# Sums of weight blocks: from VectorE to accumulating DMAs, and more pairs computed with them

## The chip, the core and the metric

The kernel runs on one core of one Trainium2 chip. The metric is the device time of one execution in microseconds (us), the median of several runs. TensorE (PE in the rows) multiplies, VectorE (DVE) and ScalarE (ACT) work element by element, GpSimd (POOL) does a few small sums and powers, and SyncE (SP) issues nearly all loads.

## The reference

Two layers of a decoder trunk over 512 tokens of width 1024. Each layer is a half-step SwiGLU, a mixing stage (sliding-window attention beside gated linear attention), and a second half-step SwiGLU. So there are four feed-forward stages, and the change is in them:

```python
def swiglu(h, w_gate, w_up, w_down):
    return (jax.nn.silu(h @ w_gate) * (h @ w_up)) @ w_down

h = rmsnorm(x, ffn1_norm[l])
x = x + 0.5 * swiglu(h, ffn1_w_gate[l], ffn1_w_up[l], ffn1_w_down[l])
...
h = rmsnorm(x, ffn2_norm[l])
x = x + 0.5 * swiglu(h, ffn2_w_gate[l], ffn2_w_up[l], ffn2_w_down[l])
```

The hidden width is 2816, that is 22 blocks of 128 columns.

## The kernel before

**Precision.** Everything is float32. TensorE is fed pairs of a rounded part and a rest: `split` has ACT round a 128x512 piece (line 112, `whi<-raw`) and DVE subtract (line 113, `wlo<-raw,whi`). `mul3` (lines 182 to 184) makes one product of three matmuls: high by high, high by low, low by high.

**The feed-forward stage.** `ffn` goes through 22 pairs `j`; a pair is 128 gate columns and 128 up columns of the weights, both over 1024 rows. Two halves, `h = 0` with pairs 0 to 10 and `h = 1` with pairs 11 to 21, are each followed by eight blocks of the down projection (`wd`). A pair is computed in one of two ways:

- `plain`: 8 row blocks, gate and up, three matmuls each: 48 matmuls with 128x512 outputs.
- `combined`: a Strassen-like scheme (Winograd's form) over rows, columns and tokens. Seven products, each of 4 row blocks and three matmuls on half of the tokens: 84 matmuls with 128x256 outputs. The activations' sums are made once per stage by `Norm.combine`; the weights' sums are made for each pair in `Combined`.

`PLAIN` names the pairs that are computed plainly: nine of 22.

**Weights of a combined pair.** `Combined` loads the pair's 128x2048 block into `raw` (two 512 KB loads on SP's queue) and cuts it in four: `g0`, `u0`, `g1`, `u1` (gate and up, even and odd row blocks). Each product needs one piece: 1 is `g0`, 2 is `g1`, 4 is `u1`, and 5, 6, 7 and 3 are sums and differences, which DVE makes in place inside `raw` by four tensor instructions (lines 166, 168, 171, 173). `raw` has two buffers, so the load of a pair waits until the last piece of the pair two before it has been split. `whi` and `wlo` have six buffers each: a new piece can be split only when TensorE has used up the piece six before.

**Order.** A scheduler fixes the order of the instructions on each engine when the kernel is built; a queue then runs in that order, and an instruction that waits holds up all behind it. `tc.high_priority(offset=PREP)` moves the preparation of weights ahead. TensorE's order within combined pairs is: product 1 of this pair, 4 of the pair before, 5 of this, 3 of the pair before, then 6, 2 and 7 of this. ACT copies product 1, 1+6 and 7 out (lines 363, 369, 375), takes the SiLU (line 319) and rounds the result (line 112, `q<-t` or `k<-t`); DVE adds (lines 373, 376, 383) and multiplies (386, 387).

The three lines on which most of this rests:

```python
raw = wpool.tile([P, 2048], F32, name="raw", tag="raw", bufs=2)
return [wpool.tile([P, 512], F32R, name=z, tag=z) for z in ("whi", "wlo")]
wpool = ctx.enter_context(tc.tile_pool(name="wpool", bufs=6))
```

Of the kernel before, what the change touches and what calls it, by code (L numbers as in the profile page):

```python
# [14 lines left out]
ALU = mybir.AluOpType  # L15
# [29 lines left out]

H = T // 2

PLAIN = (0, 1, 2, 3, 4, 8, 11, 15, 19)

VB = 144  # L50
VCUT = (0, 400, 784, 1168)
# [3 lines left out]
def trunk(ctx, tc, xT, wgu, wd, wqk, wv, wg, wpa, wpb, wo, glaw, vecs, consts, masks, out):  # L55
# [91 lines left out]
    class Combined:  # L147
# [3 lines left out]
        def __init__(self, src):  # L151
            self.of = {}

            def parts(product, r):
                self.of[product] = piece()
                split(*(z.rearrange("p (k c) -> p k c", k=4) for z in self.of[product]), r)

            with tc.high_priority(offset=PREP):
                raw = wpool.tile([P, 2048], F32, name="raw", tag="raw", bufs=2)
                for c in range(0, 2048, 1024):  # L160
                    nc.sync.dma_start(raw[:, c:c + 1024], src[:, c:c + 1024])

                r = raw.rearrange("p (k a n c) -> p k a n c", k=4, a=2, n=2)
                g0, u0, g1, u1 = (r[:, :, a, n, :] for a in range(2) for n in range(2))
                parts(1, g0)
                V.tensor_add(u0, u0, u1)
                parts(5, u0)
                V.tensor_sub(g0, u0, g0)
                parts(6, g0)
                parts(2, g1)  # L170
                V.tensor_sub(u0, u1, g0)
                parts(7, u0)
                V.tensor_sub(g1, g1, g0)
                parts(4, u1)
                parts(3, g1)

        def at(self, product, pair):
            return [z[:, pair * P:pair * P + P] for z in self.of[product]]
# [28 lines left out]
    class Norm:  # L207
# [14 lines left out]
        def whole(self, d):  # L222

            if d % 2 == 0:
                self.w = slot(f"{sets[1]}{d // 2}", (P, 2, T))
            t = self.w[:, d % 2, :]
            V.scalar_tensor_tensor(t, x[d], col(self.l, self.vcol + d), self.rb, op0=ALU.mult, op1=ALU.mult)  # L227
            split(*self.u[d], t)
            self.full.append(t)

        def combine(self, n):

            a, b = 2 * n, 2 * n + 1
            a0, a1, b0, b1 = (self.full[z][:, c:c + H] for z in (a, b) for c in (0, H))
            t, s = temp(2), temp(2)
            V.tensor_sub(t[:, :H], a1, a0)  # L236
            V.tensor_sub(t[:, H:], b1, t[:, :H])  # L237
            V.tensor_sub(s[:, :H], b1, a1)  # L238
            V.tensor_sub(s[:, H:], b0, t[:, H:])
            if n < 3:  # L240
                tags = (("b0", "b1"), ("qr0", "qr1"), ("ga", "gb"))[n]
                to = [[z[:, i, :] for i in range(2)] for z in (slot(v, (P, 2, T), F32R) for v in tags)]
            else:
                to = [[slot(v, dtype=F32R) for v in tags] for tags in (("attn0", "ke0"), ("attn1", "ke1"))]
            split(*to[0], t)
            split(*to[1], s)
            first, second = slice(0, H), slice(H, T)
            self.c.append({1: [z[:, first] for z in self.u[a]], 2: [z[:, first] for z in self.u[b]],
                           3: [z[:, second] for z in self.u[b]], 4: [z[:, second] for z in to[1]],
                           5: [z[:, first] for z in to[0]], 6: [z[:, second] for z in to[0]],  # L250
                           7: [z[:, first] for z in to[1]]})
# [40 lines left out]
    def ffn(f, norm, nxt, spill, last):  # L292
        for h in range(2):
            g = []

            rest = []
            room = {}

            def left(n=2):
                while n and rest:  # L300
                    rest.pop(0)()
                    n -= 1

            def part(tag, n):

                if tag not in room:
                    room[tag] = slot(tag, (P, 2, T), F32R)
                return room[tag][:, n, :]

            def keep(j, tu):  # L310
                if j < 8:
                    hi, lo = slot(f"{'qk'[j % 2]}{j // 2}", dtype=F32R), part(f"v{j // 2}", j % 2)
                else:
                    hi, lo = (part(f"{sets[1]}{2 * z + (j - 8) // 2}", j % 2) for z in range(2))
                split(hi, lo, tu)
                g.append((hi, lo))

            def silu(to, z):
                tables[0] = S.activation(to, z, AF.Silu)

            def plain(j):
                raw = h == 0 and j < 3
                w = first if f + h + j == 0 else Weights(wgu[f, h * NH + j], KD, 256)
                pg, pu = acc(), acc()
                for k in range(KD):
                    if h == 0 and j == 1 and k == 2:
                        norm.scale()
                    if h == 0 and j == 1 and k == 6:
                        norm.spread()
                    if k in (2, 5):  # L330
                        left(1)
                    mul3(pg, w.at(k, 0, P), norm.u[k], k == 0, k == KD - 1)
                    mul3(pu, w.at(k, P, P), norm.u[k], k == 0, k == KD - 1)
                    if h == 0 and j == 2:
                        norm.whole(k)
                    if h == 0 and j in (3, 4) and k in (3, 7):
                        norm.combine(2 * j - 6 + k // 4)

                def gated():
                    tg, tu = temp(1), temp(2)  # L340
                    if raw:
                        V.tensor_mul(tg, pg, norm.rb)
                        V.tensor_mul(tu, pu, norm.rb)
                        silu(tg, tg)
                        V.tensor_mul(tu, tu, tg)
                    else:
                        silu(tg, pg)
                        V.tensor_mul(tu, pu, tg)  # L348
                    keep(j, tu)

                return gated

            def combined(j):
                w = Combined(wgu[f, h * NH + j])

                def run(to, n, start=False):
                    for k in range(4):
                        mul3(to, w.at(n, k), norm.c[k][n], start and k == 0, k == 3, not start)

                a = acc()[:, :H]  # L360
                run(a, 1, True)
                s12 = temp(1)
                S.copy(s12[:, :H], a)
                left(1)
                b = acc()[:, :H]
                run(b, 5, True)
                left(1)
                run(a, 6)
                S.copy(s12[:, H:], a)
                c = psum()[:, :H]  # L370
                run(c, 2, True)
                tg, su = temp(1), temp(2)
                V.tensor_add(tg[:, :H], c, s12[:, :H])
                run(a, 7)
                S.copy(su[:, :H], a)
                V.tensor_add(su[:, H:], b, su[:, :H])

                def up():
                    run(a, 4)

                def gate():
                    run(b, 3)
                    V.tensor_add(tg[:, H:], b, s12[:, H:])
                    silu(tg, tg)
                    tu = temp(2)
                    V.tensor_mul(tu[:, :H], a, tg[:, :H])
                    V.tensor_mul(tu[:, H:], su[:, H:], tg[:, H:])
                    keep(j, tu)

                rest.extend((up, gate))  # L390

            late = None
            for j in range(NH):
                if h * NH + j in PLAIN:
                    gated = plain(j)
                    if h == 0 and j == 0:
                        late = gated
                    else:
                        if late is not None:
                            late()  # L400
                            late = None
                        gated()
                else:
                    combined(j)
            left()
            for d in range(KD):
                w = Weights(wd[f, h, d], NH, P)
                ps = acc()
                for k in range(NH):
                    mul3(ps, w.at(k, 0, P), g[k], k == 0, k == NH - 1)  # L410
                V.scalar_tensor_tensor(x[d], ps, 0.5, x[d], op0=ALU.mult, op1=ALU.add)
                if h == 1:
                    if nxt is not None:
                        nxt.add(d)
                    if spill or last:
                        nc.sync.dma_start((xs if spill else out)[:, d, :], x[d])
# [545 lines left out]
```

## Time and profile before

| what | us |
|---|---|
| median of 3 runs (lowest, highest) | 2362.51 (2360.87, 2363.26) |
| the profiled execution | 2362.52 |
| its span in the trace | 2360.7 |
| PE busy in the span | 2340.2 |
| DVE busy | 1514.8 |
| ACT busy | 1117.7 |
| POOL busy | 157.6 |

The span is what the trace shows of one execution; the profiled execution's own time is 1.8 us longer. A busy time counts what the engine's instructions took, without waiting. The matmuls are pipelined, so the time that one is worth is the distance between two starts and not its listed duration.

### The profile page before, as it was taken

The numbers are of one execution on the slowest core, as the hardware profiler recorded it, in microseconds if no ns is written. First come the engines' busy times: TensorE is split into PE (matmuls) and PEld (weight loads), VectorE is DVE, ScalarE is ACT, GpSimd is POOL, SyncE is SP. The second block draws the span as 40 slices with busy tenths as digits, with TensorE's granted clock in tenths as the row PEclk, the third lists the DMA queues.
The fourth block names the chain that finished last, engine by engine and source line by source line (L and its number), as shares of the span: only waits on it lengthen the run. The fifth ranks groups of instructions, "written<-read, shape, count | busy, mean of one in ns | idle before, by whom it ended". The sixth has DMA issues, their size and how long they took to land. (4 is left out here: it accounts for less than half of the span.)

```text
span 2360.7 us, 33980 instructions
## 1 busy us (share of the span) xinstructions
PE 2340.2 (99%) x12904; PEld 2015.2 (85%) x12904; DVE 1514.8 (64%) x2769; ACT 1117.7 (47%) x2093; POOL 157.6 (7%) x147
## 2 busy tenths in 40 slices
PE   9999999999999999999999999999999999999999
PEld 7889988788888889899889899887888888898997
DVE  6846754658655678467468467456686556773772
ACT  5534544554465345345445345444544554552451
POOL 1000010003110100000100000100140101000000
PEclk9999999999999999999999999999999999999999
DMA  4232234211223322322322322431202233223222
GB/s 168 84 105 102 101 122 123 75 63 37 71 90 114 118 89 85 122 90 94 112 90 84 122 90 96 144 111 55 79 19 80 100 116 116 81 100 111 94 98 90
DMA packets 73587, 226.68 MB, mean 96 GB/s; under 512 B 8720, under 2 KB 16912, under 8 KB 73424
## 3 DMA queue, kind: packets, MB, share of 16 engines
q1 hardware_dynamic: 71136, 221.46, 27.7%
q10 hardware_dynamic: 2288, 3.06, 0.5%
q8 instruction: 101, 1.65, 0.3%
q14 instruction: 62, 0.51, 0.1%
HBM read 215.58 MB, written 6.29 MB: 94 GB/s over the span
## 5 line engine op out<-in xcount | busy, mean ns | idle before, releaser
L112 ACT CAST whi<-raw 128x512 fp32r<-128x512 f32 (+2 forms) x976 | 589.0, 608 | 922.2 <-PE mm L183 795.0
L113 DVE TENSOR_TENSOR wlo<-raw,whi 128x512 fp32r<-128x512 f32 (+2 forms) x976 | 668.0, 688 | 504.3 <-ACT whi L112 494.0
L182 PE MATMUL mm<-uh,whi 128*128 128x512 f32 (+1 forms) x1584 | 580.2, 366 | 5.5 <-ACT uh L218 5.4
L184 PE MATMUL mm<-uh,wlo 128*128 128x512 f32 (+1 forms) x1584 | 577.7, 365 | 1.9 <-DVE wlo L113 1.6
L183 PE MATMUL mm<-ul,whi 128*128 128x512 f32 (+1 forms) x1584 | 577.6, 365 | 0.0
L184 PEld LDWEIGHTS mm<-uh,wlo 128*128 128x128 f32 x1584 | 300.1, 190 | 50.5 <-DVE wlo L113 5.7
L182 PEld LDWEIGHTS mm<-uh,whi 128*128 128x128 f32 x1584 | 300.6, 190 | 49.8 <-ACT uh L218 5.4
L183 PEld LDWEIGHTS mm<-ul,whi 128*128 128x128 f32 x1584 | 300.7, 190 | 44.5 <-DVE ul L219 0.5
L183 PE MATMUL mm<-v,whi 128*128 128x512 f32 x640 | 249.1, 389 | 0.0
L183 PEld LDWEIGHTS mm<-v,whi 128*128 128x128 f32 x640 | 120.2, 188 | 24.4
L182 PE MATMUL mm<-k,whi 128*128 128x512 f32 x320 | 124.6, 389 | 0.0
L182 PE MATMUL mm<-q,whi 128*128 128x512 f32 x320 | 124.5, 389 | 0.0
L184 PE MATMUL mm<-k,wlo 128*128 128x512 f32 x320 | 124.5, 389 | 0.0
L184 PE MATMUL mm<-q,wlo 128*128 128x512 f32 x320 | 124.5, 389 | 0.0
L264 POOL TENSOR_TENSOR sum<-sum,t 128x512 f32<-128x512 f32 x39 | 53.5, 1373 | 681.6 <-ACT t L263 385.9
L182 PE MATMUL mm<-b,whi 128*128 128x256 f32 (+1 forms) x272 | 85.9, 316 | 0.1
L182 PE MATMUL mm<-qr,whi 128*128 128x256 f32 (+1 forms) x272 | 83.7, 308 | 0.0
L184 PE MATMUL mm<-qr,wlo 128*128 128x256 f32 (+1 forms) x272 | 83.7, 308 | 0.0
L184 PE MATMUL mm<-b,wlo 128*128 128x256 f32 (+1 forms) x272 | 83.7, 308 | 0.0
L183 PE MATMUL mm<-o,whi 128*128 128x512 f32 x192 | 75.1, 391 | 0.0
L183 PE MATMUL mm<-x,whi 128*128 128x512 f32 x192 | 75.1, 391 | 0.0
L196 ACT ACTIVATE t<-t 128x512 f32<-128x512 f32 (+1 forms) x72 | 43.4, 608 | 64.9 <-DVE t L656 60.2
(326 smaller groups left out, 4268.7 us busy)
## 6 DMA issues: line engine op xcount, KB each, us to landing
raw<-in_wgu SPq DMA_DIRECT2D x174, 512.0 KB, 4.0
raw<-in_wd SPq DMA_DIRECT2D x64, 512.0 KB, 3.5
raw<-in_wg SPq DMA_DIRECT2D x48, 512.0 KB, 4.4
raw<-in_wqk SPq DMA_DIRECT2D x26, 512.0 KB, 4.4
raw<-in_wd SPq DMA_DIRECT2D x64, 192.0 KB, 3.7
raw<-in_wpb SPq DMA_DIRECT2D x16, 512.0 KB, 4.2
raw<-in_wo SPq DMA_DIRECT2D x16, 512.0 KB, 6.0
raw<-in_wv SPq DMA_DIRECT2D x16, 384.0 KB, 3.5
```

The lines of the kernel that those rows point to most:

```text
L112: S.copy(hi, src)
L113: V.tensor_sub(lo, src, hi.bitcast(F32))
L182: PE.matmul(ps, w[0], a[0], start=start, stop=False, skip_group_check=onto)
L183: PE.matmul(ps, w[0], a[1], start=False, stop=False, skip_group_check=onto)
L184: PE.matmul(ps, w[1], a[0], start=False, stop=stop, skip_group_check=onto)
L196: after(S.activation(*args, **kw), tables[1])
L264: G.tensor_tensor(self.sum, self.sum, sq, op=ALU.add)
```

## The change

The four sums of weights are no longer made by DVE. They are made by DMAs on GpSimd's queue that read a 256 KB block of the weights from device memory and add it to a block of `raw` (`accum_op=ALU.add`). All of them add; the differences are turned into sums: the activations that meet combined pairs are negated when they are split (`Norm.whole`), one of `combine`'s differences is turned around, and the signs are taken back in the SiLU's scale and in the multiplication by it. The host lays the block out so that each quarter is contiguous. And `PLAIN` holds only pairs 0 to 4: 17 of 22 pairs are combined in place of 13.

```diff
-PLAIN = (0, 1, 2, 3, 4, 8, 11, 15, 19)
+PLAIN = (0, 1, 2, 3, 4)
...
-                r = raw.rearrange("p (k a n c) -> p k a n c", k=4, a=2, n=2)
-                g0, u0, g1, u1 = (r[:, :, a, n, :] for a in range(2) for n in range(2))
+                (g0, u0, g1, u1), (dg0, du0, dg1, du1) = ([z[:, c:c + 512] for c in range(0, 2048, 512)]
+                                                          for z in (raw, src))
+
+                def plus(to, what):
+                    nc.gpsimd.dma_start(to, what, accum_op=ALU.add)
+
                 parts(1, g0)
-                V.tensor_add(u0, u0, u1)
+                plus(u0, du1)
                 parts(5, u0)
-                V.tensor_sub(g0, u0, g0)
-                parts(6, g0)
+                plus(u0, dg0)
+                plus(g0, du0)
+                parts(6, u0)
                 parts(2, g1)
-                V.tensor_sub(u0, u1, g0)
-                parts(7, u0)
-                V.tensor_sub(g1, g1, g0)
+                plus(u0, dg1)
+                parts(7, g0)
                 parts(4, u1)
-                parts(3, g1)
+                parts(3, u0)
...
-            split(*self.u[d], t)
+
+            hi, lo = self.u[d]
+            S.activation(hi, t, AF.Copy, scale=-1.0)
+            V.scalar_tensor_tensor(lo, t, -1.0, hi.bitcast(F32), op0=ALU.mult, op1=ALU.subtract)
...
-            V.tensor_sub(s[:, :H], b1, a1)
+            V.tensor_sub(s[:, :H], a1, b1)
...
-            def silu(to, z):
-                tables[0] = S.activation(to, z, AF.Silu)
+            def silu(to, z, scale=-1.0):
+                tables[0] = S.activation(to, z, AF.Silu, scale=scale)
...
-                        silu(tg, tg)
+                        silu(tg, tg, 1.0)
...
-                        V.tensor_mul(tu, pu, tg)
+                        V.scalar_tensor_tensor(tu, pu, -1.0, tg, op0=ALU.mult, op1=ALU.mult)
```

Three places in the order show what moved. The number behind `raw_` names the pair. A pair's seven pieces are split in the order of its products 1, 5, 6, 2, 7, 4, 3, and the number behind `whi_` rises in that order.

DVE before, in the first stage, at the pair `raw_898`: pieces 1, 5, 6, 2, 7 and 4 (line 113), two of the sums in place (168, 171) and a third (173) between them.

```order
L113 TENSOR_TENSOR wlo_902<-raw_898,whi_901 128x512
L113 TENSOR_TENSOR wlo_907<-raw_898,whi_906 128x512
L168 TENSOR_TENSOR raw_898<-raw_898 128x4x128
L386 TENSOR_TENSOR t2_849<-mm_689,t1_743 128x256
L171 TENSOR_TENSOR raw_898<-raw_898 128x4x128
L113 TENSOR_TENSOR wlo_912<-raw_898,whi_911 128x512
L387 TENSOR_TENSOR t2_849<-t2_744,t1_743 128x256
L113 TENSOR_TENSOR wlo_916<-raw_898,whi_915 128x512
L113 TENSOR_TENSOR wlo_921<-raw_898,whi_920 128x512
L173 TENSOR_TENSOR raw_898<-raw_898 128x4x128
L113 TENSOR_TENSOR wlo_926<-raw_898,whi_925 128x512
```

In the changed kernel these in-place instructions are gone from DVE, and GpSimd's queue holds the sums. There, at the pairs `raw_1175` and `raw_1314` of the same stage, the rows are: the second and third sums of `raw_1037` (`g0 += u0` and `u0 += g0`), the first of `raw_1175` (`u0 += u1`), the last of `raw_1037` (`u0 += g1`), then the same for the next two pairs.

```order
L166 DMA raw_1037<-in_wgu 128x512 x2
L166 DMA raw_1175<-in_wgu 128x512
L166 DMA raw_1037<-in_wgu 128x512
L166 DMA raw_1175<-in_wgu 128x512 x2
L166 DMA raw_1314<-in_wgu 128x512
L166 DMA raw_1175<-in_wgu 128x512
```

So the first sum of a pair stands ahead of the last sum of the pair before it.

ACT in the changed kernel, from pieces 2 and 7 of `raw_1175` on: copy of product 1 (line 369), pieces 4 and 3, then pieces 1 and 5 of the next pair with a SiLU (325) between, two copies and a rounded result, and that pair's piece 6.

```order
L112 CAST whi_1193<-raw_1175 128x512
L112 CAST whi_1198<-raw_1175 128x512
L369 COPY t1_1223<-mm_1210 128x256
L112 CAST whi_1202<-raw_1175 128x512
L112 CAST whi_1206<-raw_1175 128x512
L112 CAST whi_1317<-raw_1314 128x512
L325 ACTIVATE t1_1158<-t1_1158 128x512
L112 CAST whi_1322<-raw_1314 128x512
L375 COPY t1_1223<-mm_1210 128x256
L112 CAST o0_1267<-t2_1264 128x512
L381 COPY t2_1298<-mm_1210 128x256
L112 CAST whi_1328<-raw_1314 128x512
```

Pieces 5, 6, 7 and 3 now wait for a DMA where they waited for DVE, and all pieces of a pair stand on ACT ahead of the first piece of the next pair.

## Rows read from the trace of the kernel before

**Rows 1.** Page, busy us (share of span) and instructions by engine.

```profile
PE 2340.2 (99%) x12904; PEld 2015.2 (85%) x12904; DVE 1514.8 (64%) x2769; ACT 1117.7 (47%) x2093; POOL 157.6 (7%) x147
```

**Rows 2.** Busy time by window: a combined pair; a combined with a plain pair.

```profile
core 0: us, PE busy (x) PEld busy (x) DVE busy (x) ACT busy (x) POOL busy (x), PEclk, DMA share, GB/s
215.70:225.78 10.08, 10.08 (x86) 10.08 (x86) 8.76 (x16) 6.28 (x13) 0.00 (x0) 1.00 0.33 104
225.78:249.84 24.06, 24.06 (x159) 22.12 (x159) 17.80 (x32) 12.12 (x23) 0.00 (x0) 1.00 0.26 89
```

**Rows 3.** Timeline, PE: start, duration, engine; from combined to plain matmuls.

```profile
233.53 0.28 PE L183 MATMUL mm<-ke,whi 128*128 128x256 f32 x1
233.65 0.28 PE L184 MATMUL mm<-attn,wlo 128*128 128x256 f32 x1
233.77 0.40 PE L182 MATMUL mm<-uh,whi 128*128 128x512 f32 x1
234.01 0.40 PE L183 MATMUL mm<-ul,whi 128*128 128x512 f32 x1
234.24 0.39 PE L184 MATMUL mm<-uh,wlo 128*128 128x512 f32 x1
234.47 0.40 PE L182 MATMUL mm<-uh,whi 128*128 128x512 f32 x1
```

**Rows 4.** Timeline, ACT: one combined pair, from product 1 to product 1.

```profile
215.70 0.37 ACT L363 COPY t<-mm 128x256 f32<-128x256 f32 x1
216.57 0.62 ACT L112 CAST whi<-raw 128x512 fp32r<-128x512 f32 x1 [0.50 <-PE mm L183]
218.06 0.62 ACT L112 CAST whi<-raw 128x512 fp32r<-128x512 f32 x1 [0.86 <-PE mm L183]
219.45 0.62 ACT L112 CAST whi<-raw 128x512 fp32r<-128x512 f32 x1 [0.78 <-PE mm L183]
...
225.78 0.37 ACT L363 COPY t<-mm 128x256 f32<-128x256 f32 x1
```

**Rows 5.** Groups by line and shape, whole run: busy, mean ns, idle before.

```profile
L113 DVE TENSOR_TENSOR wlo<-raw,whi 128x512 fp32r<-128x512 f32 x864 | 605.8, 705 | 472.1 <-ACT whi L112 462.3
L168 DVE TENSOR_TENSOR raw<-raw 128x512 f32<-128x512 f32 x52 | 35.8, 688 | 1.1
...
L112 ACT CAST whi<-raw 128x512 fp32r<-128x512 f32 x864 | 531.4, 620 | 797.8 <-PE mm L183 703.0 <-issue 24.7 <-ACT t L375 14.3
L319 ACT ACTIVATE t<-t 128x512 f32<-128x512 f32 x64 | 40.4, 632 | 1.0 <-DVE t L342 0.8
```

**Rows 6.** DMA issues: queue, count, KB each, median us to landing.

```profile
raw<-in_wgu SPq DMA_DIRECT2D x174, 512.0 KB, 4.0
...
o<-xs SPq DMA_DIRECT2D x8, 256.0 KB, 3.1
...
t<-o ACTq DMA_DIRECT2D x20, 64.0 KB, 2.0
...
raw<-in_wgu SPq DMA_DIRECT2D x4, 256.0 KB, 5.3
```

**Rows 7.** The sixteen 256 KB loads of line 803 (`o<-xs`, `x<-xs`).

```profile
DMA to landing us min/median/max: 2.9/3.1/4.0
```

**Rows 8.** All loads into `raw`.

```profile
DMA to landing us min/median/max: 3.0/4.0/7.8
```

**Rows 9.** Busy time by window, columns as in rows 2: 128x1 matmuls, then wide ones.

```profile
24.00:28.00 4.00, 4.00 (x25) 3.98 (x25) 0.32 (x2) 0.00 (x0) 0.08 (x1) 0.67 0.68 227
28.00:32.00 4.00, 4.00 (x11) 3.05 (x10) 0.45 (x1) 0.00 (x0) 1.33 (x1) 0.50 0.00 0
32.00:36.00 4.00, 4.00 (x23) 3.45 (x21) 0.85 (x2) 1.24 (x2) 0.00 (x0) 0.98 0.31 104
```

More of the change, by code (lines that the diff above doesn't have):

```diff
@@ L155, in parts @@
                 self.of[product] = piece()
-                split(*(z.rearrange("p (k c) -> p k c", k=4) for z in self.of[product]), r)
+                split(*self.of[product], r)
             with tc.high_priority(offset=PREP):
@@ L899 @@
             for f in range(NF):
-                wgu[2 * l + n, f] = _blocks(gu, [(f * P, f * P + P), (FF + f * P, FF + f * P + P)])
+                z = _blocks(gu, [(f * P, f * P + P), (FF + f * P, FF + f * P + P)])
+                if f not in PLAIN:
+                    z = z.reshape(P, 4, 2, 2, P).transpose(0, 2, 3, 1, 4).reshape(P, 2048)
+                wgu[2 * l + n, f] = z
             for h in range(2):
```

## The prediction, written before the changed kernel was run

> **What bounds the kernel now.** I read the busy times of the engines first. PE is busy for 2340.2 of 2360.7 us [rows 1], so the next question is whether it runs at its rate inside the combined pairs or waits there. The windows and the timeline answer it. In a run of combined pairs, the copy of product 1 comes every 10.08 us [rows 4]. A pair is 84 matmuls, so 0.12 us each, and that is the distance between two 128x256 matmuls that follow each other closely [rows 3]. PE loses nothing there: it is the bound. A combined and a plain pair together take 24.06 us [rows 2]; 10.08 us of that are the combined pair's, and 24 more matmuls (products 4 and 3 of the pair before) take 2.88, so a plain pair is 11.10 us, 48 matmuls at 0.23 [rows 3]. DVE is next in line: 8.76 us busy in that pair's 10.08 [rows 2], 2.8 of it the four sums at 0.69 [rows 5]. The preparation has some air: ACT's casts of weights sit for 0.5 to 0.9 us until PE frees a piece [rows 4], 703 us in all [rows 5].
>
> **Part 1: four more combined pairs in each of four stages.** 16 pairs x (11.10 - 10.08) = 16.3 us less on PE, if PE stays the bound. Each adds three casts on ACT and three subtractions on DVE, beside PE's work; DVE has room for them by part 2.
>
> **Part 2: the sums leave DVE.** 52 pairs x 4 x 0.69 us = 143 us of DVE work go. As PE waits for almost none of it today, this alone gives nothing; it lets combined pairs follow each other with DVE at some 6 us in 10.08. The negated split and the scaled SiLU keep their number of instructions and their shapes: nothing.
>
> **Part 3: the sums become transfers in a chain.** This decides. A sum on DVE began when the subtraction ahead of it had ended. A sum by DMA has to be issued after the last read of what it overwrites, lands some us later, and the cast that needs it stands at the head of ACT's queue until then, with everything behind it. Follow `u0`: split as piece 5; `u0 += g0` is issued when DVE has finished that piece; ACT casts piece 6 when it has landed; `u0 += g1` is issued when DVE has finished piece 6; ACT casts piece 3 when that has landed; and only behind piece 3 does the order let ACT cast pieces 1 and 5 of the next pair. So preparation can't run ahead over the waits: per pair there is one loop,
> cast 3 (0.62) + cast 1 (0.62) + SiLU (0.63) + cast 5 (0.62) + subtraction (0.69) + landing L + cast 6 (0.62) + subtraction (0.69) + landing L = 4.5 us + 2L [rows 5].
> The other instructions on ACT (copies, pieces 2, 7 and 4) fit inside the two waits. PE needs 10.08 us per pair, so the loop is hidden up to L = 2.8 us; beyond that every 0.1 us of landing costs 0.2 us a pair.
>
> **The price L.** No row shows a DMA on GpSimd's queue, nor one that accumulates. From below: a plain 256 KB load from device memory on SP's queue lands in 2.9 to 4.0 us, median 3.1 [rows 6, 7]; an accumulating one reads the same bytes and the destination too, and I see no reason for it to land earlier. From above: 5.3 us for 256 KB loads into `raw` while other loads were in flight [rows 6]. The loads of the next pairs (1 MB each, 3.0 to 7.8 us [rows 8]) do run beside the sums here. I take 4.0 us, the row of the 512 KB loads [rows 6], as a sum moves 256 KB in and has 256 KB of destination to read. Then the loop is 12.5 us, 2.4 us more than PE's pair.
>
> *How often.* A stage has a run of 6 and one of 11 combined pairs. At the start of each, up to six pieces are ready ahead, 8.6 us of work at 1.44 us a product, and the wait has to eat the slack first; I take two pairs of each run as covered. That leaves 13 pairs a stage, 52 in all: 52 x 2.4 = 125 us. With the gain of part 1: **+109 us, 2362.5 + 109 = 2471 us** on the profiled execution, whose own time is that of the median. PE waits late in the runs, mostly for product 1 (behind piece 3 of the pair before) and product 6.
>
> At the bounds: L = 3.1 gives a loop of 10.7, 0.6 x 52 - 16 = +15, 2378 us. L = 5.3 gives 15.1 us, 5.0 us a pair, with one pair of each run covered 60 x 5.0 - 16 = +284, 2646 us.
>
> **Other queues.** GpSimd's queue was nearly empty (157.6 us busy [rows 1]) and the norms' sums on it lie outside the runs of combined pairs. But the first sum of the next pair stands ahead of `u0 += g1` on it, and waits for a load that starts only when piece 3 of the pair before last has been split: 4.0 (load) + L + 0.62 + 0.69 = 9.3 us, under the loop of 12.5. At the slowest load, 7.8 us [rows 8], it is 13.1, a loop of its own of the same size.
>
> **A rule of the Trainium skill against the change.** In the trace the subtraction of line 113 reads two operands and is DVE's largest group, 605.8 us [rows 5]. The Trainium skill, GPSIMD Engine Reference, section Specifications, says that GpSimd's interface to SBUF is shared with VectorE, with contention when a DVE instruction has two SBUF inputs; by that, the making of the descriptors could be held up to 0.69 us at a time, and twice that in the loop would be 72 us more over 52 pairs. No row here shows it, and it is not in the sum.
>
> **Rivals.**
> *The sums land in time.* If L is below 2.8 us, PE stays the bound and the whole gain of part 1 arrives: 2362.5 - 16.3 = 2346 us. The tipping point is L = 2.95, where 52 waits of 0.3 us eat the 16.3. For it: 64 KB between two places on chip take 2.0 us [rows 6], so the fixed part is small. Against it: not one of 16 plain loads of the same size was under 2.9 [rows 7], and the sums have more to do. By the Trainium skill, DMA: Bandwidth & Descriptors, section Anatomy of one DMA, a DMA from GpSimd's queue takes about 2.0 us plus its bytes at 436 GB/s; that is an estimate of 2.6 us for 256 KB, and by it this rival would hold. The trace's plain loads, 3.1 us, lie above that figure. I give it 0.14.
> *It cancels.* L of 2.9 to 3.0 leaves the time within 0.2% (4.7 us, about what a measurement here can tell from no change). 0.06.
> *Much slower.* L of 5 us and more by crowding with the loads, or PE's clock falling: after some 4 us in which PE did only 128x1 matmuls, it was granted half speed, 1.2 instead of 2.4 GHz, for 4 us of wide matmuls [rows 9]. The forecast's gaps are shorter and have full matmuls between them. 2600 us and more. 0.15.
> The forecast's own case, L between 3 and 5 us: 0.65.
>
> **How the numbers follow.** The likeliest case gives 2471. Faster is the first rival, 0.14; same 0.06; slower 0.65 + 0.15 = 0.80. The range runs from 2350, so that it takes in the cancelling and a part of the first rival, to 2620, L about 5.
>
> **What would show it.** Right: in the stretches of combined pairs the copies of product 1 come some 12.5 us apart, not 10.08; ACT's casts of pieces wait for DMAs and no longer for PE; PE's idle time is put down to the subtractions of line 113; the new DMAs take about 4 us to land; DVE is some 100 us less busy. Plain pairs, the mixing stage and the down projections keep their times. Wrong: copies 10.08 us apart with landings under 2.8 us; or a stall outside the runs of combined pairs, which the loop does not explain.

## The result, and the profile of the changed kernel

The changed kernel took 2673.07 us (median of 4 runs, 2670.01 to 2677.61) against 2361.84 for the kernel before: a ratio of 1.1321, 95% interval 1.1307 to 1.1334. The prediction was 2471 us with a range up to 2620. It had the sign and lies 202 us short, outside its own range.

The profiled execution took 2673.27 us, its span 2671.5. Page, busy us (share of span) and instructions by engine, which answers [rows 1]:

```profile
PE 2434.5 (91%) x13480; PEld 2125.2 (80%) x13480; DVE 1426.0 (53%) x2673; ACT 1141.7 (43%) x2189; POOL 393.1 (15%) x419
```

PE was busy for 99% of the span and now sits idle for 237 us. It also has 94 us more busy time although Part 1 took matmul work away: part of it ran at a lower clock (granted 0.957 over the run, 0.998 before). DVE is 89 us less busy.

The same page, DMA queues (packets, MB, share of the 16 engines' span) and issues (KB each, median us to landing). It answers [rows 6]:

```profile
q1 hardware_dynamic: 71136, 221.46, 25.3%
q0 software_dynamic: 39168, 71.32, 15.6%
...
raw<-in_wgu SPq DMA_DIRECT2D x174, 512.0 KB, 4.5
raw<-in_wgu POOLq DMA_DIRECT2D x272, 256.0 KB, 5.2
```

q0 is GpSimd's queue, which was empty before. A sum lands after 5.2 us in the median. Line 166 of the changed kernel, the sums:

```profile
L166 POOL DMA_DIRECT2D raw<-in_wgu x272: 856/865/1215, 49.7 to 2594.6; - x136
...
DMA to landing us min/median/max: 3.5/5.2/7.7
```

Busy time by window, columns as in [rows 2]: the six combined pairs of the first stage's first half, then the down projections behind them, then the eleven combined pairs.

```profile
72.00:148.00 76.00, 61.08 (x427) 59.45 (x426) 36.96 (x70) 31.55 (x64) 15.83 (x19) 0.87 0.57 128
148.00:221.00 73.00, 70.91 (x343) 60.27 (x343) 29.63 (x51) 21.36 (x39) 4.93 (x6) 0.98 0.42 119
221.00:375.00 154.00, 118.81 (x844) 115.35 (x843) 65.87 (x125) 57.13 (x116) 32.89 (x38) 0.89 0.60 132
```

PE is idle for a fifth of the time in the combined runs (14.9 of 76 us, 35.2 of 154) and for 2.1 of 73 between them; the granted clock is 0.87 and 0.89 in the runs, 0.98 between them. In the whole run, some 218 of PE's 237 idle us lie in the eight runs of combined pairs. The loss is where the sums are.

Waits of the whole run, largest first (engine, line, what it waited for: us, times, longest):

```profile
DVE wlo L113 <- ACT whi L112: 870.3, 408, 6.6
...
ACT whi L112 <- PE mm L186: 562.9, 324, 8.9
ACT whi L112 <- DMA raw<-in_wgu: 463.0, 131, 6.4
...
PE mm L185 <- ACT t L375: 168.7, 60, 4.9
...
PE mm L185 <- ACT t L369: 45.6, 40, 3.0
```

ACT's casts wait 463 us for DMAs, where all readers of `raw` together had waited 14 us for them before. PE waits most for ACT's copy of product 1+6 (line 375), once in nearly every pair, and then for the copy of product 1 (line 369): 214 of its 237 idle us.

One loop shows how the one leads to the other. Timeline of ACT from piece 3 of a pair to piece 3 of the next, which answers [rows 4]; "x2" and "x3" are casts in a row, here pieces 3, 1, 5, then 6, 2, 7, then 3 and 1:

```profile
268.86 1.66 ACT L112 CAST whi<-raw 128x512 fp32r<-128x512 f32 x3 [2.88 <-DMA raw<-in_wgu]
271.17 0.63 ACT L325 ACTIVATE t<-t 128x512 f32<-128x512 f32 x1 [0.65 <-DVE t L389]
271.71 0.35 ACT L375 COPY t<-mm 128x256 f32<-128x256 f32 x1
...
275.08 0.37 ACT L381 COPY t<-mm 128x256 f32<-128x256 f32 x1 [1.84 <-PE mm L187]
279.30 1.66 ACT L112 CAST whi<-raw 128x512 fp32r<-128x512 f32 x3 [3.84 <-DMA raw<-in_wgu]
280.87 0.36 ACT L369 COPY t<-mm 128x256 f32<-128x256 f32 x1
...
284.65 1.14 ACT L112 CAST whi<-raw 128x512 fp32r<-128x512 f32 x2 [2.91 <-DMA raw<-in_wgu]
```

and GpSimd's issues beside it: the third sum (`g0 += u0`) and the second (`u0 += g0`) one behind the other in this order, the first of the next pair, the last.

```profile
271.10 1.80 POOL L166 DMA_DIRECT2D raw<-in_wgu  x2 [5.06 <-DVE wlo L113]
274.85 0.86 POOL L166 DMA_DIRECT2D raw<-in_wgu  x1 [1.95 <-DMA raw<-in_wgu]
280.94 0.86 POOL L166 DMA_DIRECT2D raw<-in_wgu  x1 [5.22 <-DVE wlo L113]
```

From piece 3 (268.86) to the issue of `u0 += g0` (272.04 in the trace, the second of the two) are 3.18 us; piece 6 is cast 7.26 us after that issue (279.30); 1.64 us later `u0 += g1` is issued (280.94); the next piece 3 is cast 3.71 us after that (284.65). The sum is 15.79 us, the loop that the prediction wrote down, with larger numbers in it. Matched one by one over the whole run, issue to landing has a median of 5.0 us for the first sum of a pair, 6.1 for the second, 6.0 for the third and 3.6 for the last (68 each).

The copy of product 1+6 at 271.71 stands on ACT's queue behind the cast of piece 3 that waited 2.88 us, and PE had nothing to do meanwhile. Timeline of PE there (start, duration), the end of product 2, then product 7, which is added onto the copied sum, and the products behind it:

```profile
268.36 0.28 PE L187 MATMUL sm<-uh,wlo 128*128 128x256 f32 x1
272.12 0.58 PE L185 MATMUL mm<-b,whi 128*128 128x256 f32 x1 [3.48 <-ACT t L375]
272.50 0.41 PE L186 MATMUL mm<-b,whi 128*128 128x256 f32 x1
272.71 0.41 PE L187 MATMUL mm<-b,wlo 128*128 128x256 f32 x1
...
277.54 0.28 PE L186 MATMUL mm<-b,whi 128*128 128x256 f32 x1
277.67 0.28 PE L187 MATMUL mm<-b,wlo 128*128 128x256 f32 x1
```

After the stall two matmuls are 0.21 us apart, and from 277.4 on again 0.12 [rows 3]: 5.3 us at the lower of the two clock levels (1.2 GHz), then the higher.

**A measure used below.** Copies of product 1 come 68 times, with 60 distances inside runs of combined pairs. In the changed kernel the first distance of each of the eight runs is 10.9 to 11.9 us, the other 52 have a mean of 15.45. PE's own pace is 7.2 for a first and 10.08 for the others. A distance tells when the copy came; PE can have work in hand while a copy is late.

### The profile page after: what moved, and what is told of

Read it like the earlier page. It is cut to its first block, busy times and chain, and to the rows that moved or that the text cites. A ratio compares the mean times of both kernels' runs of the same rounds, so it can differ in the third digit from the quotient of the medians.

```text
span 2671.5 us, 35780 instructions
## 1 busy us (share of the span) xinstructions
PE 2434.5 (91%) x13480; PEld 2125.2 (80%) x13480; DVE 1426.0 (53%) x2673; ACT 1141.7 (43%) x2189; POOL 393.1 (15%) x419
## 3 DMA queue, kind: packets, MB, share of 16 engines
q0 software_dynamic: 39168, 71.32, 15.6%
## 4 chain that ended last, share of the span: by engine, by line
PE 31%; DMA 9%; issue 6%; DVE 3%; ACT 2%; POOL 2%; ACTq 0%; POOLq 0%; DVEq 0%
PE mm L185 9%; PE mm L186 9%; PE mm L187 9%; DMA raw<-in_wgu 9%; POOL raw L166 1%; ACT whi L112 1%; DVE wlo L113 1%; PE sm L678 1%; PE mm L523 0%; PE mm L525 0%; PE mm L524 0%; PE sm L616 0%; PE sm L585 0%; PE sm L609 0%; ACT t L199 0%
## 5 line engine op out<-in xcount | busy, mean ns | idle before, releaser
L185 PE MATMUL mm<-uh,whi 128*128 128x512 f32 (+1 forms) x1456 | 532.6, 366 | 6.0 <-ACT uh L221 6.0
L186 PE MATMUL mm<-ul,whi 128*128 128x512 f32 (+1 forms) x1456 | 530.4, 364 | 0.0
L187 PE MATMUL mm<-uh,wlo 128*128 128x512 f32 (+1 forms) x1456 | 528.2, 363 | 0.9 <-DVE wlo L113 0.7
L166 POOL DMA_DIRECT2D raw<-in_wgu x272 | 235.7, 870 | 1140.0 <-DVE wlo L113 724.9
L185 PE MATMUL mm<-b,whi 128*128 128x256 f32 (+1 forms) x336 | 120.8, 359 | 214.7 <-ACT t L375 168.7
L185 PEld LDWEIGHTS mm<-b,whi 128*128 128x128 f32 x336 | 69.6, 207 | 240.2 <-ACT t L375 180.9
L187 PE MATMUL mm<-b,wlo 128*128 128x256 f32 (+1 forms) x336 | 107.4, 320 | 0.0
L187 PE MATMUL mm<-qr,wlo 128*128 128x256 f32 (+1 forms) x336 | 106.9, 318 | 0.0
L185 PE MATMUL mm<-qr,whi 128*128 128x256 f32 (+1 forms) x336 | 106.8, 318 | 0.0
L186 PE MATMUL mm<-ke,whi 128*128 128x256 f32 x272 | 83.5, 307 | 3.0 <-DVE ke L113 3.0
```

Of the source, the lines that this page charges most:

```text
L166: nc.gpsimd.dma_start(to, what, accum_op=ALU.add)
L185: PE.matmul(ps, w[0], a[0], start=start, stop=False, skip_group_check=onto)
L186: PE.matmul(ps, w[0], a[1], start=False, stop=False, skip_group_check=onto)
L187: PE.matmul(ps, w[1], a[0], start=False, stop=stop, skip_group_check=onto)
```

## Experiments

The theory with this result in view: the loop of the prediction is there, with larger landings, and sets the pace of the preparation. Rivals: the sums cost something wherever they stand (the queue, or the memory they load); the change has another cost than the sums; the six pieces ahead don't cover what the prediction thought.

### The other part alone: 17 pairs, sums on DVE

Edit of the kernel before:

```diff
-PLAIN = (0, 1, 2, 3, 4, 8, 11, 15, 19)
+PLAIN = (0, 1, 2, 3, 4)
```

> Part 1 alone: 17 of 22 pairs combined, the sums stay on DVE as in the kernel before. Theory (what slows the change is the loop of two landings per pair, 15.4 us in its trace against 10.08 us of PE; nothing else): PE stays the bound, 16 pairs x 1.02 us less, 2346 us, copies of product 1 about 10.1 us apart. Rival (17 combined pairs can't be prepared in time whoever makes the sums): DVE with 7 subtractions and 4 sums a pair falls behind, 2362 us or more, copies 10.5 us apart and wider.

Measured: 2352.89 us, ratio 0.9968 (0.9956 to 0.998), between the theory and the rival. Copies come mostly 10.08 us apart in the second halves; in the first halves, where DVE still works on the norm, they are 7.7 to 11.7 apart. Part 1 is a gain, but only half of the 16.3 us arrives. From the first copy of a stage's first half to that of its second are 123.4 to 123.6 us, against 120.5 in the kernel without sums below: 12 us in four stages, lost where DVE is busy.

### Short runs: the old nine plain pairs, sums by DMA

```diff
-PLAIN = (0, 1, 2, 3, 4)
+PLAIN = (0, 1, 2, 3, 4, 8, 11, 15, 19)
```

> Parts 2 and 3 alone: the sums by DMA with the old list of plain pairs, 13 of 22 combined, in runs of 3 and 2. Theory (loop of 15.4 us per pair, only as far as pieces ahead and a plain pair's 11.1 us between don't cover it): a run of three and a plain pair needs 3 x 15.4 + 4 casts of the plain pair 2.5 = 48.7 us against 41.3 on PE, 7.4 us lost, a run of two 2 us; 3 x 7.4 + 2 x 2 = 26 us a stage, 105 us in all, 2467 us at most and some 20 us less where pieces ahead cover it. Rival (each sum by DMA costs its share wherever it stands): 327 us x 208/272 sums = 250 us more, 2612 us.

Measured: 2577.79 us, ratio 1.0922 (1.0902 to 1.0942), over 100 us above the theory and nearer the rival: 217 us over before on 52 combined pairs, 4.2 us each, although all runs of combined pairs are only two or three pairs long. Waits:

```profile
ACT whi L112 <- DMA raw<-in_wgu: 370.1, 97, 7.7
...
PE mm L185 <- ACT t L375: 100.1, 32, 5.5
```

The step "two pairs of each run are covered by the pieces ahead" falls: if two were free, the 12 third pairs would have to cost 18 us each. The rival, that a sum costs its share wherever it stands, is answered by the runs with one sum below.

### No sums at all

The same kernel with the four DMAs left out, so the products take unsummed weights.

```diff
-                    nc.gpsimd.dma_start(to, what, accum_op=ALU.add)
+                    pass
```

> The changed kernel without its accumulating DMAs: the sums of weights are left out, the pieces are split from the block as it was loaded. Theory: without landings in the loop PE is the bound, 2346 us, and copies of product 1 are 10.08 us apart. Rival (the rest of the change, order, layout, negated split or 17 pairs, is slow by itself): more than 2360 us.

Measured: 2336.91 us, ratio 0.99 (0.9886 to 0.9913), copies 10.08 us apart (9.8 to 10.4) behind the first distance of each run. All of the 336 us between this and the changed kernel hang on the sums. It is also 24 us under before, where Part 1 had 16.3. Most of the other 8 can be estimated from the copies. From the first copy of a stage's first half to the first of its second half are 134.4 us before; five combined pairs, two plain ones and the 60.05 us of the down projections (120.53 here, less six pairs) make 132.65. So the kernel before already lost some 7 us in four first halves, where DVE held PE up.

### Plain copies in place of accumulations

The DMAs overwrite `u0` and `g0` instead of adding, on the same queue at the same places.

```diff
-                    nc.gpsimd.dma_start(to, what, accum_op=ALU.add)
+                    nc.gpsimd.dma_start(to, what)
```

> The changed kernel with the same 272 transfers on GpSimd's queue, each a plain copy: nothing is added. The order of instructions is the same on every engine. Theory (the landing is long because an accumulating packet takes 178 ns for 2 KB, 1.74 us a sum, and the sums stand behind a load): a copy of 256 KB takes about half, so the landing of the second sum falls by some 0.85 us for itself and as much for the one ahead of it, the last by 0.85: loop 15.4 - 2.5 = 12.9 us, 60 x 2.8 - 16 = +152, 2515 us. Rival (the price is GpSimd's queue itself, the issue of 0.87 us and the start of 1.6 us): little change, 2640 us or more.

Measured: 2506.02 us, ratio 1.0618 (1.0598 to 1.0637), as the theory expected. Its page and its line 166:

```profile
q0 software_dynamic: 21760, 71.32, 8.0%
...
raw<-in_wgu POOLq DMA_DIRECT2D x272, 256.0 KB, 3.4
```

The same bytes take 8.0% of 2500.5 us on the 16 DMA engines, 0.74 us per transfer, against 15.6% of 2671.5, 1.53 us, when they accumulate. The landing falls from 5.2 to 3.4 in the median (the second sum's from 6.1 to 4.2, the last's from 3.6 to 3.25), and the mean of the 60 distances from 14.93 to 12.48 us. So the loop holds with shorter landings too, and accumulation is worth 167 us. In that is its longer issue: GpSimd takes 0.87 us for one in the median, 0.54 for a plain copy.

### Half of the loads

Only 512 KB of each combined block are loaded; pieces 2 and 4 are split from the first quarter, so their products are of other weights.

```diff
-                for c in range(0, 2048, 1024):
-                    nc.sync.dma_start(raw[:, c:c + 1024], src[:, c:c + 1024])
+                nc.sync.dma_start(raw[:, :1024], src[:, :1024])
...
+                g1 = u1 = g0
```

> The changed kernel with half of the load ahead of the sums: of each combined pair's block only the first 512 KB are loaded, and pieces 2 and 4 are split from the first block instead of their own (so the products 2 and 4 are not the reference's). All 272 sums stay. Theory (the second sum lands late, 6 us against 3.75 us for the last, because the 1 MB load that piece 3 sets off runs ahead of it on the same DMA engines for 4.8 us): half the load frees some 2 us of that wait, the loop falls from 15.4 to about 13.3 us, 2337 + 63 x 3.2 = 2540 us. Rival (GpSimd's queue and its own transfers hold the second sum, not the load): within 20 us of 2672.

Measured: 2632.81 us, ratio 1.1148 (1.1125 to 1.117); sums land in 4.8 us in the median, the second in 5.3 in place of 6.1, the last in 3.8. Halving the load is worth 40 us of the 336, a third of what the theory expected, and twice what the rival allowed; for what remains of the second sum's excess over the last's the trace offers the third sum, which stands ahead of it in the queue.

### Piece 3 cast later

Piece 3 is split behind pieces 1 and 5 of the next pair, to take one of the two landings out of the loop.

```diff
...
                 parts(5, u0)
+                for step in later:
+                    step()
+                later[:] = [lambda: parts(3, u0)]
...
-                parts(3, u0)
...
```

> The changed kernel with one thing reordered: piece 3 of a pair is split behind pieces 1 and 5 of the next pair. All sums by DMA, 17 pairs. Theory (a loop over two landings in a row, because piece 3 stands ahead of the next pair's pieces): the second sum of the next pair is issued before piece 3 waits, so the two landings run side by side, and ahead of the load that piece 3 sets off; the loop has one landing, 4.5 + some 6 = 10.5 to 11.5 us, 2337 + 63 x (0.4 to 1.4) = 2362 to 2425 us. The transfers alone (four sums at 1.74, a load at 2.6 to 4.8) take 9.6 to 11.8 us a pair, so it can hardly be better. Rival (every wait for a sum stalls PE by itself, since the copies out of PSUM stand behind it on ACT, whatever the loop): four waits a pair as before, 2550 us or more.

Measured: 2679.31 us, ratio 1.1349 (1.133 to 1.1368), far above the expected range. ACT's timeline there:

```profile
299.92 0.62 ACT L112 CAST whi<-raw 128x512 fp32r<-128x512 f32 x1 [4.25 <-DMA raw<-in_wgu]
...
300.97 0.60 ACT L112 CAST whi<-raw 128x512 fp32r<-128x512 f32 x1
...
305.80 1.14 ACT L112 CAST whi<-raw 128x512 fp32r<-128x512 f32 x2 [3.22 <-DMA raw<-in_wgu]
```

Piece 5 (299.92) now waits for the first sum, and piece 6 (305.80) for the second. The reading: `raw` has two buffers, so the load of the pair after starts only when piece 3 (300.97) has been split; its halves land at 307.14 and 308.41 in the trace. The first sum of that pair is issued at 308.02, behind the last sum of the pair before (307.44), and lands at 313.15; piece 5 of that pair, which waits for it, is cast at 313.25, ahead of the next piece 3. (A matmul freed the buffer for this piece at 313.18, so it would have waited as long for PE here.) From piece 5 to piece 5 are 13.33 us here, with a landing of 5.1 in them; the first sum before it took 6.4 (293.40 to 299.81). So the edit took a landing out of one loop and closed another with a load and a landing in it, which the expectation overlooked. That is read from the trace; a third buffer for `raw` would test it, and was not tried.

### Only the first sum by DMA

`u0 += u1` stays a DMA, the other three go back to DVE. This sum waits for the pair's load and for nothing that ACT or DVE does.

```diff
                 plus(u0, du1)
                 parts(5, u0)
-                plus(u0, dg0)
-                plus(g0, du0)
+                V.tensor_add(u0, u0, g0)
                 parts(6, u0)
+                V.tensor_sub(g0, u0, u1)
                 parts(2, g1)
-                plus(u0, dg1)
+                V.tensor_add(u0, u0, g1)
```

> 17 pairs, but only the first sum (u1 onto u0) by DMA, which waits for no piece; the other three on DVE. Theory (what costs is a sum that has to wait for a piece to be split, inside the loop): no landing is left in the loop, PE stays the bound, 2337 to 2346 us, faster than the kernel before by 0.6 to 1%. Rival (a sum by DMA costs where it stands, since it lands behind the loads): product 5's piece is late, 1 us or more a pair, 2400 us or more.

Measured: 2341.42 us, ratio 0.9913 (0.9898 to 0.9928), as the theory expected, and faster than both kernels, though only 0.9% under the one before. Line 166 and the waits:

```profile
DMA to landing us min/median/max: 3.5/3.8/4.9
```

```profile
ACT whi L112 <- PE mm L186: 733.5, 592, 7.3
```

No wait of ACT for a sum is listed; the casts wait for PE again, and copies come 10.02 to 10.09 us apart, 7.2 or 8.0 at a run's start. A landing of 3.8 us that lies outside the loop costs next to nothing: 4.5 us over the kernel with no sums at all.

### First and third sum by DMA

```diff
-                plus(u0, dg0)
+                V.tensor_add(u0, u0, g0)
                 plus(g0, du0)
...
-                plus(u0, dg1)
+                V.tensor_add(u0, u0, g1)
```

> As the run with one sum by DMA, and the third sum (u0 onto g0, issued after piece 1 and needed for piece 7) by DMA too; two sums on DVE. Theory: the loop has no landing, but piece 7 comes some 6 us after piece 1 and the sum between them lands in 4 to 6 us if it stands behind a load, so small waits at most: 2340 to 2375 us. Rival: as before, 2450 us or more.

Measured: 2485.11 us, ratio 1.0529 (1.0512 to 1.0545): above the expected range, as the rival said. ACT's timeline, from piece 6 to piece 7 of a pair and to the next piece 7:

```profile
297.29 0.62 ACT L112 CAST whi<-raw 128x512 fp32r<-128x512 f32 x1 [0.78 <-DVE raw L171]
...
303.78 1.66 ACT L112 CAST whi<-raw 128x512 fp32r<-128x512 f32 x3 [1.99 <-DMA raw<-in_wgu]
...
316.73 1.66 ACT L112 CAST whi<-raw 128x512 fp32r<-128x512 f32 x3 [4.57 <-DMA raw<-in_wgu]
```

The third sum overwrites `g0`, which DVE's sum of line 171 reads; that sum comes only after piece 5. I had taken it for one that waits for piece 1 alone, as in the changed kernel. But line 171 is not what held it last. GpSimd's queue has the first sum of the next pair ahead of it, and that one waits for its pair's load. In 50 of the 60 distances the two are issued one behind the other, the first of them 0.56 to 0.65 us after the load has landed. In the loop shown: pieces 7, 4 and 3 are cast from 303.78 on, the last of them sets off a load at 306.35, which lands at 310.20; the next pair's first sum is issued at 310.76, the third sum at 311.30, and that lands at 316.65 for the cast at 316.73. These 12.95 us hold a load and a landing. The distances have a mean of 12.0 us. So a sum that waits for a load alone is not free where a sum that ACT waits for stands behind it in the queue.

### Only the last, only the second

Two kernels with one DMA each inside the loop: `u0 += g1` alone, and `u0 += g0` alone. The diff of the first, and the lines of the second that differ from it:

```diff
-                plus(u0, du1)
+                V.tensor_add(u0, u0, u1)
...
-                plus(u0, dg0)
-                plus(g0, du0)
+                V.tensor_add(u0, u0, g0)
...
+                V.tensor_sub(g0, u0, u1)
...
                 plus(u0, dg1)
```

```diff
-                V.tensor_add(u0, u0, g0)
+                plus(u0, dg0)
...
-                plus(u0, dg1)
+                V.tensor_add(u0, u0, g1)
```

> 17 pairs combined; only the last sum of a pair (u0 += g1) is a DMA, the other three stay on DVE. It is issued when DVE has finished piece 6 and piece 3 waits for it; between the two stand pieces 2, 7 and 4 and two copies on ACT, 2.6 us. The loop is 4.5 us + 0.69 for the sum that DVE makes + some 0.3 to the issue + one landing. With the 3.75 us that such a landing took in the changed kernel it is 9.3 us, under PE's 10.08, and the copy of 1+6 still comes in time. Theory (the loop of landings sets the period): 2337 to 2352 us, copies of product 1 10.08 us apart. Rival (any landing that ACT waits for stalls PE at once, through the copies behind it, wherever the sum stands): 2 us a pair and more, 2450 us and above.

Measured: 2364.24 us (10 runs), ratio 1.0009 (1.0 to 1.0019). It is 12 us above the range of the theory and far from the rival. ACT's timeline: piece 4, then 3 and 1 of the next pair, then the SiLU:

```profile
296.07 0.62 ACT L112 CAST whi<-raw 128x512 fp32r<-128x512 f32 x1 [0.50 <-PE mm L186]
298.77 1.14 ACT L112 CAST whi<-raw 128x512 fp32r<-128x512 f32 x2 [2.08 <-DMA raw<-in_wgu]
300.48 0.63 ACT L325 ACTIVATE t<-t 128x512 f32<-128x512 f32 x1 [0.57 <-DVE t L389]
```

ACT waits 2.08 us for the landing and then 0.57 for DVE, which the expectation left out. The loop is some 10.4 us, 0.3 over PE's pair: from piece 3 to the issue are 6.57 us (288.42 to 294.99 in the trace) in place of the expected 5.5, and 3.78 from the issue to the next piece 3, as expected.

> 17 pairs combined; only the second sum (u0 += g0) is a DMA, the other three stay on DVE. It is issued when DVE has finished piece 5, some 2.7 us after piece 3 has set off the 1 MB load of the pair after next, so that its packets come behind the load's. In the changed kernel that landing was 6 us and more, with two other sums in the queue too; alone behind the load I expect 5.5. Theory: the loop is 4.5 + 0.69 + 0.3 + 5.5 = 11.0 us, 0.9 over PE's pair, 68 pairs: 2337 + 62 = 2400 us, range 2370 to 2430. Rival A (the load in front costs nothing; a landing is 3.75): the loop is 9.3 us, 2337 to 2352. Rival B (the stalled copies add a price of their own to each pair): 2450 and above.

Measured: 2409.48 us, ratio 1.0203 (1.0188 to 1.0218). The time is in the expected range, by luck: two terms were off and cancel.

```profile
298.92 1.66 ACT L112 CAST whi<-raw 128x512 fp32r<-128x512 f32 x3 [2.56 <-DMA raw<-in_wgu]
...
301.58 1.14 ACT L112 CAST whi<-raw 128x512 fp32r<-128x512 f32 x2 [0.21 <-DVE raw L175]
303.65 0.63 ACT L325 ACTIVATE t<-t 128x512 f32<-128x512 f32 x1 [0.92 <-DVE t L389]
...
310.04 1.66 ACT L112 CAST whi<-raw 128x512 fp32r<-128x512 f32 x3 [2.82 <-DMA raw<-in_wgu]
```

Piece 6 comes 11.12 us after piece 6. The landing was 3.8 us in the median, not 5.5; the way from piece 6 to the issue (305.97 in the trace) was 7.05 us, not 5.5, with the waits for DVE (0.21 and 0.92) and the copies in it.

### What they say together

| sums by DMA | of them waited for inside the loop | mean distance of copies, us | time, us |
|---|---|---|---|
| none, left out | 0 | 9.70 | 2336.9 |
| none, all on DVE | 0 | 9.91 | 2352.9 |
| first | 0 | 9.74 | 2341.4 |
| last | 1 | 10.02 | 2364.2 |
| second | 1 | 10.97 | 2409.5 |
| first and third | 1 (the third), and a load | 12.00 | 2485.1 |
| all four, as copies | 2 | 12.48 | 2506.0 |
| all four, half of the load | 2 | 14.12 | 2632.8 |
| all four, accumulating | 2 | 14.93 | 2673.1 |
| all four, piece 3 later | 1 (the first), and a load | 14.96 | 2679.3 |

The time follows all that stands in the loop, not the count of waits alone. One DMA of the same 256 KB a pair costs 5, 27 or 73 us over no sums, by which sum it is; so its bytes do not set the price.

## Why the prediction was right or wrong

**What bounds the kernel: right.** With the sums gone, copies come at PE's 10.08 us, and the time falls by what the pairs save and some 8 us more.

**Part 1, 16.3 us: right in sign and roughly in size.** 24 us with no sums, 20 with only the first sum by DMA, 8 with all sums on DVE.

**Part 2, nothing by itself: nearly.** DVE is 89 us less busy in a kernel that is slower. But the 11 us between all sums on DVE and the first one moved off it, most of them in the first halves of the stages, show that DVE did hold PE back once more pairs were combined. "PE waits for almost none of it today" was a little off too: the kernel before lost some 7 us there, by the estimate above.

**Part 3, the loop: right in kind.** ACT waits for the DMAs, PE waits for what stands behind on ACT, and the plain stretches nearly keep their pace (74.3 to 74.7 us from the last copy of a first half to the first of the second, 73.0 with no sums). In the runs of combined pairs ACT's casts wait some 430 us for DMAs and some 40 for PE, where it was some 200 for PE before. PE's idle time is put down to ACT's copies (line 375), though, not to the subtractions of line 113 that the prediction named.

**The size of the loop: too small in both terms.** Predicted 12.5 us for 52 pairs, measured 15.45 in the 52 distances behind the first ones: 52 x 2.95 = 153 us of the miss.

- The landings were 2 x 4.0 us and are 6.1 + 3.6 = 9.7 in the median: 1.7 us a pair, 88 us. The last sum, with nothing ahead of it, is even under 4.0; the second is over the upper bound of 5.3.
- The fixed part was 4.5 us; what is left of 15.45 is 5.75: 1.25 us a pair, 65 us. In the loop shown it is 3.18 + 1.64 = 4.8, with some 0.3 us from a subtraction's end to an issue and the third sum's 0.9 us of issuing in front of the second's landing; in the next loop the SiLU stands in it too and waits for DVE.
- Why the second sum is late: an accumulation keeps the DMA engines busy for twice as long as a copy of its bytes (1.53 against 0.74 us), and the prediction had no more than its 4.0 us for a sum beside a load and other sums. In the loop shown, piece 3 sets off a 1 MB load ahead of the sums. By the DMA records its packets run from 271.19 to 275.53, and those of the three sums, issued at 271.10, 272.04 and 274.85, from 274.77 to 280.16; the third sum lands at 277.15, the second at 279.22. The prediction looked at who stands ahead of `u0 += g1` on GpSimd's queue; the place that mattered was ahead of `u0 += g0`.

**"Two pairs of each run are covered by six pieces ahead": wrong, it was one.** The first distance of a run is long (11.5 us in place of 7.2), but PE lost little in it: its gaps there sum to 0.1 to 0.4 us, those in the second distance to 3.4 to 5.3 in each of the eight runs. So eight more pairs paid, 8 x 5.37 = 43 us that were costed at nothing. Timeline of ACT at the start of a run of eleven:

```profile
222.93 0.37 ACT L369 COPY t<-mm 128x256 f32<-128x256 f32 x1
...
227.97 0.37 ACT L381 COPY t<-mm 128x256 f32<-128x256 f32 x1 [2.11 <-PE mm L187]
233.02 1.66 ACT L112 CAST whi<-raw 128x512 fp32r<-128x512 f32 x3 [4.68 <-DMA raw<-in_wgu]
...
238.35 1.14 ACT L112 CAST whi<-raw 128x512 fp32r<-128x512 f32 x2 [2.88 <-DMA raw<-in_wgu]
...
241.10 0.36 ACT L375 COPY t<-mm 128x256 f32<-128x256 f32 x1
```

and of PE, at product 7 of the second pair:

```profile
237.85 0.28 PE L187 MATMUL sm<-uh,wlo 128*128 128x256 f32 x1
241.52 0.39 PE L185 MATMUL mm<-b,whi 128*128 128x256 f32 x1 [3.39 <-ACT t L375]
```

Already piece 6 of the second pair waits 4.68 us. The step that failed is a half sentence: "the other instructions on ACT (copies, pieces 2, 7 and 4) fit inside the two waits". In time they do. But a queue runs in order, so the copies stand behind a wait, and PE needs them: product 6 is added onto the copied product 1, product 7 onto the copied sum. Here piece 7 had been cast by 234.7 (the third of the three from 233.02 on), but the copy stood behind the wait for piece 3 and came at 241.10. Pieces that are ready help PE no further than the next copy. That is read from the traces; no run moved the copies.

So the sum reads: 2337 (no sums) + 322 (60 pairs x 5.37) + 14 that were not traced = 2673. The prediction's was 2346 + 125 (52 pairs x 2.4).

**The rivals.** "The sums land in time" fell: no sum landed in under 3.5 us, where the point of decision was 2.95. "Much slower", given 0.15, is what came: crowding and long landings, and the granted clock fell too, though the prediction took its gaps for too short for that: in the loop shown it is at the lower level from 270.60 on, inside a gap of PE of 3.48 us. How much of the 336 us is the clock's was not measured apart. In the loop shown, ACT waited 3.84 us for a DMA behind the copy at 275.08, the last instruction that had waited for PE, so a faster PE would have gained nothing there.

**The estimate of the landing, and the shared interface.** The Trainium skill, DMA: Bandwidth & Descriptors, section Anatomy of one DMA, gave an estimate of 2.6 us for 256 KB on GpSimd's queue; plain copies there landed in 2.9 at least and 3.4 in the median, accumulating ones in 3.5 at least and 3.8 in the median with only one to a pair. The measurement decides, and it lies on the other side of the tipping point. The Trainium skill, GPSIMD Engine Reference, section Specifications, speaks of contention between GpSimd and VectorE when a DVE instruction has two SBUF inputs. By the rows of line 166 an issue took GpSimd 865 ns in the median and 1215 at most, 862 and 1056 with only the first sum by DMA, where DVE is busier (67%). In the changed kernel, 135 issues had the subtraction of line 113 running for over half of their time and 85 not at all; the median is 865 ns for both. There is no sign of the 72 us that the prediction worked out as a possible extra.

## What to carry to other kernels

Before work is moved from an engine to a DMA, find what the DMA has to wait for and which queue waits for it: one that waits for nothing but a load can land late for free, if nothing that is waited for stands behind it in its own queue; one that needs an engine's last result and feeds that engine's next instruction puts its whole landing into the loop. An instruction that waits holds up all that follows in its queue, so list those that another engine needs soon (here the copies out of the accumulators), before you count buffers as cover. For a kind of transfer that the trace doesn't show, cost the loop at the upper bound as well as at the likely one, and put every wait for another engine into its fixed part.

## What was unexpected about the hardware

- A DMA that accumulates keeps the DMA engines busy for 1.53 us per 256 KB in the mean, a plain copy on the same queue 0.74. Its packets are of 2 KB where the copy's are of 4, and one takes 178 ns in the median, the copy's 159. With nothing ahead of it, it landed in 3.6 us, the plain copy in 3.25 (medians of the last sum).
- An issue takes GpSimd 0.87 us when it accumulates and 0.54 when it copies, and in the DMA records the first packet of a sum that nothing stood ahead of came 1.6 us after the issue began (280.94 to 282.51).
- The sums and the load, though issued on different engines' queues, share the DMA engines. In the loop shown, 268.86 to 284.65 us (packets, MB, share of 16 engines):

```profile
q0 software_dynamic: 576, 1.05, 38.3%
q1 hardware_dynamic: 288, 1.05, 21.2%
```

  Four sums take 6.0 of these 15.8 us and the 1 MB load 3.3, for the same bytes, and the sums' packets came when the load was nearly through. The Trainium skill, DMA: Bandwidth & Descriptors, section Issuing engines are not separate DMA queues, says that DMAs of all issuing engines run on the same 16 DMA engines and interleave; the trace agrees on the sharing, and in this stretch shows little of the interleaving.
